# Mixing the state-space tiles of a group in one insertion, with the last keys in 64 masked rows and the root a step later

## The chip, the cores and the metric

One NeuronCore of a Trainium2 chip runs the kernel; the others are idle. The metric is the device time of one execution in microseconds (us), the median of several runs. TensorE (PE) multiplies into PSUM, VectorE (DVE) and ScalarE (ACT) do the elementwise work, GpSimd (POOL) sets constants up, and SyncE (SP) issues the DMAs that bring weights in.

## The reference

A two-layer trunk over 272 tokens (16 learned meta tokens ahead of 256) and a width of 2048. Layer 0 is a Mamba-2 mixer and a SwiGLU; layer 1 is a stick-breaking attention against a shared K/V and a SwiGLU. The change touches only the mixer's scan, which per chunk of the sequence computes

```python
cum = jnp.cumsum(dtc * A, axis=1)
seg = cum[:, :, None] - cum[:, None, :]
decay = jnp.exp(jnp.where(causal, seg, -jnp.inf))
cb = jnp.einsum("bqgn,bsgn->bqsg", cc, bc)
xdt = xc * dtc[..., None]
y_diag = jnp.einsum("bqsg,bqsgr,bsgrp->bqgrp", cb, decay, xdt)
y_off = jnp.einsum("bqgn,bgrpn->bqgrp", cc, state) * jnp.exp(cum)[..., None]
```

There are 8 groups of 8 heads of 64 channels, with a state of 128. Behind the scan each group is multiplied by a gate, divided by the root of its mean square (the "root" below) and sent through an output projection.

## The kernel before, in words

Everything is kept transposed, channels in partitions and tokens in the free dimension. A projection (`project`, L130) makes 128 output channels for all 272 tokens: it loads a piece of 8 weight blocks of 128x128 (`load`, L94, on SP's queue, 5 buffers), splits it into a rounded half `hi` on ScalarE (L105, 5 buffers) and the remainder `lo` on VectorE (L107, 4 buffers), and runs three matmuls of 272 columns per block (L120, L121, L122). With 16 blocks that is 48 matmuls, with the 8 blocks of an output projection 24. The result lies in one of four `pp` buffers of PSUM until VectorE takes it away (L163, or L166 for the residual).

The mixer's eight groups run one after another. `ssd_project` (L328) makes a group's six convolution tiles (B, C and four tiles of x; a projection, taps at L321 and L324, a Silu at L326) and four gate tiles `zs`. The scan itself, `ssd_scan` (L357), is a generator: it is put on a list, and `pump` (L196) runs it up to its next `yield` after each projection of the *next* group or, behind groups 3 and 5 and behind the last one, of an output projection. A group's projections give ten such steps. Within this, the Tile framework's scheduler decides the order in which each engine's instructions stand; each engine then runs its own list strictly in that order.

A scan's steps for a group (272 tokens in key blocks of 128, 128 and 16; the queries that a block reaches are `QRY`):

1. Loads of the decay's exponents (`et`, `elast`, `ef`, L379 and L398); the scores `pc` (L400 to L402); twelve transposes of the x tiles (L367), four for each key block, the last block's being 16 wide; the causal mask (L405 to L407).
2. to 5. The keys times their step size (`scaled`, L370), the decay by Relu and Exp on ScalarE (L386, L421 to L424), decay times scores (`mix`, L388).
6. and 7. The products, two of the four tiles in each step (L435): for a tile, four matmuls of a 64-wide half with 128 and 144 query columns and two with the 16 columns of the last keys (L440), which add up in one PSUM tile `py`, then one 128-wide matmul for the part of the carried state (L442). VectorE adds the parts and multiplies with the gate (L444 to L450), ScalarE squares (L177, L180), VectorE sums the squares in `ga` (L181).
8. The root: a matmul with ones (L188) that sums `ga` over partitions, Sqrt on ScalarE, a reciprocal on VectorE (L191).
9. The scaled result is split into two halves `y` for the output projection (L459 to L462).

`cum` and the step size `dt` are made once, ahead of group 0, transposed on PE (L293, L294) and kept as `cumT` and `dtT`; `cum` also goes to DRAM, whence the decay's exponents are broadcast.

Of the kernel before, what the change touches and what calls it, by code (L numbers as in the profile page):

```python
# [6 lines left out]
F32 = mybir.dt.float32  # L7
F32R = mybir.dt.float32r
AF = mybir.ActivationFunctionType
ALU = mybir.AluOpType  # L10
# [3 lines left out]
P = 128  # L14
# [3 lines left out]
META = 16  # L18
T = SEQ + META
G = 8  # L20
HPG = 8
HD = 64
NH = G * HPG
DI = 4096
GT = DI // G // P
# [4 lines left out]
WC = 8  # L30
LC = 8
BLK = [(0, 128), (128, 256), (256, 272)]
QRY = [(0, 128), (128, 272), (256, 272)]
OQ = 128
SCALE = 128 ** -0.5
NEG = -1e30
# [9 lines left out]
def trunk(tc, a, out):  # L46
    nc = tc.nc
    V, S, PE = nc.vector, nc.scalar, nc.tensor

    with tc.tile_pool(name="const", bufs=1) as cp, \  # L50
# [7 lines left out]
        h = cp.tile([P, KD, T], F32, name="h")  # L58
# [6 lines left out]
        gd = cp.tile([P, 2, 32], F32, name="gd")  # L65
# [23 lines left out]
        def nm(s):  # L89
            uid[0] += 1  # L90
            return f"{s}_{uid[0]}"
# [82 lines left out]
        def sumsq(acc, src, first):  # L174
            n = src.shape[-1]
            if first:
                S.activation(acc, src, AF.Square)  # L177
            else:
                sq = sp.tile([P, T], F32, tag="sq", name=nm("sq"))
                S.activation(sq[:, :n], src, AF.Square)  # L180
                V.tensor_tensor(out=acc, in0=acc, in1=sq[:, :n], op=ALU.add)  # L181
# [48 lines left out]
        with tc.tile_pool(name="ssd0", bufs=1) as q0, \  # L230
# [6 lines left out]
                V.memset(xi[:, :CONV - 1], 0.0)  # L237
                xins.append(xi)
            cumD = dp.tile([NH, T], F32, name="cumD")
            cumT = q0.tile([P, 3, NH], F32, name="cumT")  # L240
            dtT = q0.tile([P, 3, NH], F32, name="dtT")
            wT = q0.tile([P, NH], F32, name="wT")
            ybuf = [pair(q0, 2 * GT, T, PAD["y"], TP, name=f"y{i}") for i in range(2)]

            with tc.tile_pool(name="dtp", bufs=1) as dq:
# [40 lines left out]
                for b0, b1 in ((0, OQ), (OQ, T)):  # L286
                    V.tensor_tensor_scan(cum[:, b0:b1], one[:, :b1 - b0], da[:, b0:b1],
                                         0.0, ALU.mult, ALU.add)
                nc.sync.dma_start(cumD, cum)
                pt = ptp.tile([P, 512], F32, tag="pt", name=nm("pt"))  # L290
                for b, (b0, b1) in enumerate(BLK):
                    n = b1 - b0
                    PE.transpose(pt[:n, b * NH:(b + 1) * NH], cum[:, b0:b1], ident[:NH, :NH])  # L293
                    PE.transpose(pt[:n, (3 + b) * NH:(4 + b) * NH], dt[:, b0:b1], ident[:NH, :NH])  # L294
                for b, (b0, b1) in enumerate(BLK):
                    n = b1 - b0
                    V.tensor_copy(cumT[:n, b, :], pt[:n, b * NH:(b + 1) * NH])
                    V.tensor_copy(dtT[:n, b, :], pt[:n, (3 + b) * NH:(4 + b) * NH])
                pl = prp.tile([P, 512], F32, tag="pr", name=nm("pl"))
                PE.matmul(pl[:, :NH], sel, cumT[:, 0, :], start=True, stop=True)  # L300
                V.tensor_tensor(out=wT, in0=pl[:, :NH], in1=cumT[:, 0, :], op=ALU.subtract)
# [3 lines left out]
            q1 = ctx.enter_context(tc.tile_pool(name="ssd1", bufs=1))  # L305
            q2 = ctx.enter_context(tc.tile_pool(name="ssd2", bufs=2))
            cnt = [0]
            xlast = q1.tile([P, HPG, HD], F32, name="xlast")
            elast = [q1.tile([P, HPG, META], F32, name=f"elast{i}") for i in range(2)]
            for z in (xlast, *elast):  # L310
                nc.gpsimd.memset(z, 0.0)

# [41 lines left out]
            def head_bcast(t, n, g):  # L354
                return t[:n, HPG * g:HPG * (g + 1)].unsqueeze(2).to_broadcast([n, HPG, HD])

            def ssd_scan(g, bc, xc, zs):  # L357
                gh = slice(HPG * g, HPG * (g + 1))
                xd, gm = [None] * 3, [None] * 3


                def transposed(b, pool, tag):
                    b0, b1 = BLK[b]
                    n = b1 - b0
                    pt = pool.tile([P, 512], F32, tag=tag, name=nm("pt"))
                    for j in range(GT):
                        PE.transpose(pt[:n, j * P:(j + 1) * P], xc[:, j, b0:b1], ident)  # L367
                    return pt[:n].rearrange("p (h d) -> p h d", d=HD)

                def scaled(ph, t, n, tag):  # L370
                    x = xlast if n < P else q1.tile([P, HPG, HD], F32, tag=tag, name=nm("x"))
                    V.tensor_tensor(out=x[:n], in0=ph, in1=head_bcast(t, n, g), op=ALU.mult)
                    return x

                def load_decay(b):
                    (b0, b1), (c0, c1) = BLK[b], QRY[b]
                    n = b1 - b0
                    et = elast[g % 2] if n < P else q2.tile([P, HPG, c1 - c0], F32, tag="et", name=nm("et"))
                    nc.sync.dma_start(et[:n], cumD[gh, c0:c1].partition_broadcast(n))  # L379
                    gm[b] = et  # L380


# [3 lines left out]
                        S.activation(gm[b][:, i, :], gm[b][:, i, :], AF.Relu, scale=-1.0, bias=cumT[:, b, c:c + 1])  # L386

                def mix(b):  # L388
                    n = BLK[b][1] - BLK[b][0]
                    V.tensor_tensor(out=gm[b][:n], in0=gm[b][:n],  # L390
                                    in1=cbd[b].unsqueeze(1).to_broadcast(list(gm[b][:n].shape)), op=ALU.mult)

                for b in range(3):
                    load_decay(b)
                ef = q2.tile([P, GT, T - OQ], F32, tag="ef", name=nm("ef"), bufs=1)
                cv = cumD[gh, OQ:].rearrange("(j i) q -> i j q", i=2)
                for i in range(2):
                    nc.sync.dma_start(ef[i * HD:(i + 1) * HD], cv[i].partition_broadcast(HD))  # L398
                pc = pyp.tile([P, 512], F32, tag="py", name=nm("pc"))
                PE.matmul(pc[:, 0:272], bc[:, 0, 0:128], bc[:, 1, :], start=True, stop=True)  # L400
                PE.matmul(pc[:, 272:416], bc[:, 0, 128:256], bc[:, 1, 128:], start=True, stop=True)
                PE.matmul(pc[:16, 416:432], bc[:, 0, 256:], bc[:, 1, 256:], start=True, stop=True)  # L402
                ph = [transposed(0, ptp, "pt"), transposed(1, pyp, "py"), transposed(2, prp, "pr")]
                cb = q2.tile([P, 432], F32, tag="cb", name=nm("cb"), bufs=1)
                V.tensor_tensor(out=cb[:, 0:128], in0=pc[:, 0:128], in1=causal[:, :128], op=ALU.mult)  # L405
                V.tensor_tensor(out=cb[:, 272:416], in0=pc[:, 272:416], in1=causal, op=ALU.mult)
                V.tensor_tensor(out=cb[:16, 416:432], in0=pc[:16, 416:432], in1=causal[:16, :16], op=ALU.mult)  # L407
                S.copy(cb[:, 128:272], pc[:, 128:272])
                cbd = [cb[:, 0:128], cb[:, 272:416], cb[:16, 416:432]]
                fall(0)  # L410
                yield
                xd[0] = scaled(ph[0], dtT[:, 0], P, "xd0")
                xw = scaled(ph[0], wT, P, "xw")
                fall(1)
                e2 = gm[2][:META]
                V.tensor_tensor(out=e2, in0=e2, in1=cumT[:META, 2, gh].unsqueeze(2).to_broadcast(list(e2.shape)),
                                op=ALU.subtract)
                V.tensor_scalar(e2, e2, 0.0, None, ALU.min)
                yield
                xd[1] = scaled(ph[1], dtT[:, 1], P, "xd1")  # L420
                S.activation(gm[0], gm[0], AF.Exp, scale=-1.0)  # L421
                S.activation(gm[1], gm[1], AF.Exp, scale=-1.0)
                S.activation(e2, e2, AF.Exp)
                S.activation(ef, ef, AF.Exp)  # L424
                yield
                xd[2] = scaled(ph[2], dtT[:, 2], META, "xd2")
                mix(0)
                yield
                mix(1)
                mix(2)  # L430
                yield
                ga = sp.tile([P, T], F32, tag="ga", name=nm("ga"), bufs=1)


                for j0 in range(0, GT, 2):  # L435
                    pys = [pyp.tile([P, 512], F32, tag="py", name=nm("py")) for _ in range(2)]
                    for j, py in enumerate(pys, j0):
                        for b, (c0, c1) in enumerate(QRY):
                            for i in range(2):
                                PE.matmul(py[i * HD:(i + 1) * HD, c0:c1], xd[b][:, 2 * j + i, :],  # L440
                                          gm[b][:, 2 * j + i, :], start=b < 2, stop=b != 1)
                        PE.matmul(py[:, T:T + T - OQ], xw[:, 2 * j:2 * j + 2, :], cb[:, OQ:T], start=True, stop=True)  # L442
                    for j, py in enumerate(pys, j0):
                        V.tensor_tensor(out=ef[:, j, :], in0=py[:, T:T + T - OQ], in1=ef[:, j, :], op=ALU.mult)  # L444
                        yt = q2.tile([P, T], F32, tag="yt", name=nm("yt"))
                        c = GT * g + j
                        V.scalar_tensor_tensor(out=yt, in0=xc[:, j, :], scalar=gd[:, 0, c:c + 1], in1=py[:, :T],
                                               op0=ALU.mult, op1=ALU.add)
                        V.tensor_tensor(out=yt[:, OQ:], in0=yt[:, OQ:], in1=ef[:, j, :], op=ALU.add)
                        V.tensor_tensor(out=zs[:, j, :], in0=yt, in1=zs[:, j, :], op=ALU.mult)  # L450
                        sumsq(ga, zs[:, j, :], j == 0)
                    yield
                rg = sp.tile([P, T], F32, tag="rg", name=nm("rg"), bufs=1)
                rstd(rg, ga, DI // G)
                yield
# [289 lines left out]
```

## Time and profile before

| | us |
|---|---|
| median of 3 runs | 2666.77 (2666.76 to 2666.78) |
| the profiled execution | 2667.44 |
| its span, first to last instruction | 2665.7 |
| PE busy in the span | 2648.5 |
| DVE busy | 1608.8 |
| ACT busy | 1321.5 |
| mean granted TensorE clock | 0.998 |

A row of the timeline gives start and duration in us, engine, line, operation, what is written from what, and the shape; `x8` at the end means eight records merged. An fp32 matmul shows as two records, one for each of its passes. Since matmuls overlap, a duration is longer than the distance to the next start; the distances are what PE's stream costs. A row of the waits says which instruction waited for which: us in total, times, longest. A row by line gives the busy time and the mean in ns, then the idle time ahead of these instructions and what ended it. In a form like `128*64 128x144`, the weights are 128 rows by 64 columns and 144 columns pass through them.

### The profile page before, as it was taken

To read this page: it belongs to the slowest core of one execution; us is meant where nothing else is said; L and a number is where in the kernel's file an instruction comes from. 1 tells how busy PE (TensorE), PEld (TensorE's weight loads), DVE (VectorE), ACT (ScalarE), POOL (GpSimd) and SP (SyncE) were. 2 spreads that over 40 slices of the span, in tenths; PEclk is the share of its full clock that TensorE was granted. 3 is DMA by queue.
4 is the path that set the end of the run, shared out by engine and by line. 5 is a ranking of instruction groups with operands and counts; after the bars stand their busy time and mean duration, and the time that the engine had idled before them with its cause. 6 is when DMAs were issued, how large, how long until landed. Compare 5 with 4: busy or idle time off the path is not lost.

```text
span 2665.7 us, 52272 instructions
## 1 busy us (share of the span) xinstructions
PE 2648.5 (99%) x22118; PEld 2631.8 (99%) x22118; DVE 1608.8 (60%) x2236; ACT 1321.5 (50%) x1803; POOL 5.5 (0%) x22
## 2 busy tenths in 40 slices
PE   9999999999999999999999999999999999999998
PEld 9999999999999999999999999999999999999998
DVE  8777767767765555445555665555655555554554
ACT  7777565656544443334444554444544444443443
POOL 0000000000000000000000000000000000000000
PEclk9999999999999999999999999999999999999999
DMA  6655565555555555555555555555666666665664
GB/s 226 213 178 176 173 185 173 176 177 179 164 178 178 178 179 178 179 178 180 176 179 168 184 173 156 157 163 152 196 191 192 196 193 195 193 196 180 199 198 135
DMA packets 156234, 481.23 MB, mean 181 GB/s; under 512 B 18720, under 2 KB 39776, under 8 KB 156000
## 3 DMA queue, kind: packets, MB, share of 16 engines
q1 hardware_dynamic: 155712, 477.62, 57.7%
q8 instruction: 173, 2.83, 0.4%
q14 instruction: 61, 0.50, 0.1%
q10 hardware_dynamic: 288, 0.28, 0.0%
HBM read 475.67 MB, written 2.17 MB: 179 GB/s over the span
## 4 chain that ended last, share of the span: by engine, by line
PE 96%; ACT 1%; DVE 1%; DMA 1%; issue 0%; SPq 0%; DVEq 0%; ACTq 0%
PE pp L122 31%; PE pp L121 31%; PE pp L120 31%; DMA et<-cumD 1%; PE py L440 1%; PE py L442 0%; PE pt L367 0%; ACT hi L105 0%; PE psc L569 0%; PE po L595 0%; PE po L594 0%; PE pr L188 0%; ACT et L386 0%; DVE lo L107 0%; DVE ca L324 0%
## 5 line engine op out<-in xcount | busy, mean ns | idle before, releaser
L105 ACT CAST hi<-raw 128x1024 fp32r<-128x1024 f32 (+1 forms) x899 | 928.8, 1035 | 1157.8 <-PE pp L121 928.0
L107 DVE TENSOR_TENSOR lo<-raw,hi 128x1024 fp32r<-128x1024 f32 (+1 forms) x899 | 1075.4, 1198 | 445.5 <-PE pp L122 217.4
L120 PE MATMUL pp<-u,hi 128*128 128x272 f32 (+1 forms) x4064 | 1152.2, 284 | 0.4 <-ACT hi L105 0.4
L121 PE MATMUL pp<-u,hi 128*128 128x272 f32 (+1 forms) x4064 | 1150.8, 283 | 0.0
L122 PE MATMUL pp<-u,lo 128*128 128x272 f32 (+1 forms) x4064 | 1149.1, 283 | 0.0
L120 PEld LDWEIGHTS pp<-u,hi 128*128 128x128 f32 x4064 | 764.9, 188 | 0.8 <-ACT hi L105 0.6
L121 PEld LDWEIGHTS pp<-u,hi 128*128 128x128 f32 x4064 | 764.9, 188 | 0.4
L122 PEld LDWEIGHTS pp<-u,lo 128*128 128x128 f32 x4064 | 764.4, 188 | 0.6 <-DVE lo L107 0.2
L122 PE MATMUL pp<-hid,lo 128*128 128x272 f32 (+1 forms) x1408 | 396.0, 281 | 0.0
L120 PE MATMUL pp<-hid,hi 128*128 128x272 f32 (+1 forms) x1408 | 396.0, 281 | 0.0
L121 PE MATMUL pp<-hid,hi 128*128 128x272 f32 (+1 forms) x1408 | 396.0, 281 | 0.0
L120 PEld LDWEIGHTS pp<-hid,hi 128*128 128x128 f32 x1408 | 264.8, 188 | 0.0
L121 PEld LDWEIGHTS pp<-hid,hi 128*128 128x128 f32 x1408 | 264.8, 188 | 0.0
L122 PEld LDWEIGHTS pp<-hid,lo 128*128 128x128 f32 x1408 | 264.8, 188 | 0.0
L120 PE MATMUL pp<-ukv,hi 128*128 128x272 f32 x512 | 148.2, 289 | 0.0
L120 PE MATMUL pp<-y,hi 128*128 128x272 f32 x512 | 147.6, 288 | 0.0
L121 PE MATMUL pp<-y,hi 128*128 128x272 f32 x512 | 147.1, 287 | 0.0
L122 PE MATMUL pp<-ukv,lo 128*128 128x272 f32 x512 | 146.7, 287 | 0.0
L122 PE MATMUL pp<-y,lo 128*128 128x272 f32 x512 | 146.7, 287 | 0.0
L121 PE MATMUL pp<-ukv,hi 128*128 128x272 f32 x512 | 146.7, 287 | 0.0
L166 DVE TENSOR_TENSOR h<-pp,h 128x272 f32<-128x272 f32 (+1 forms) x128 | 55.7, 436 | 118.8 <-PE pp L122 118.0
L163 DVE TENSOR_TENSOR gt<-pp,rB 128x272 f32<-128x272 f32 (+1 forms) x88 | 38.1, 433 | 135.8 <-PE pp L122 135.7
(226 smaller groups left out, 2609.8 us busy)
## 6 DMA issues: line engine op xcount, KB each, us to landing
raw<-w_gu SPq DMA_DIRECT2D x352, 512.0 KB, 3.6
raw<-w_down SPq DMA_DIRECT2D x160, 512.0 KB, 3.6
raw<-w_in SPq DMA_DIRECT2D x152, 512.0 KB, 3.7
raw<-w_out SPq DMA_DIRECT2D x64, 512.0 KB, 3.9
raw<-w_kv SPq DMA_DIRECT2D x64, 512.0 KB, 3.6
raw<-w_q SPq DMA_DIRECT2D x32, 512.0 KB, 3.6
raw<-w_o SPq DMA_DIRECT2D x32, 512.0 KB, 3.6
raw<-w_down SPq DMA_DIRECT2D x32, 256.0 KB, 2.7
```

What stands on the lines that cost most here:

```text
L105: S.copy(hi[:, :n, :m], raw[:, :n, :m])
L107: V.tensor_tensor(out=lo[:, :n, :m], in0=raw[:, :n, :m], in1=hi[:, :n, :m].bitcast(F32), op=ALU.subtract)
L120: PE.matmul(ps[:, :n], wh, xl, start=first, stop=False)
L121: PE.matmul(ps[:, :n], wh, xh, start=False, stop=False)
L122: PE.matmul(ps[:, :n], wl, xh, start=False, stop=last)
L163: V.tensor_tensor(out=dst, in0=ps[:, :r.shape[-1]], in1=r, op=ALU.mult)
L166: V.tensor_tensor(out=hm, in0=ps[:, :hm.shape[-1]], in1=hm, op=ALU.add)
L440: PE.matmul(py[i * HD:(i + 1) * HD, c0:c1], xd[b][:, 2 * j + i, :], gm[b][:, 2 * j + i, :], start=b < 2, stop=b != 1)
```

## The change

The last 16 keys no longer have 16 rows of their own. Their scores are made four times over, from keys repeated in `ke`, in 64 rows, one for each x tile and key; a mask `own` (made on GpSimd) keeps in each row only the columns of its own tile. Their x values, copied to `xe`, are transposed in one transpose to 64 rows by 128 channels. `cumR` and `dtR` hold the step sizes for these rows. So two matmuls of 64 columns make the last keys' part of all four tiles, in columns 416 to 480 of the third tile, and VectorE adds it to `ef` in one operation.

All four tiles of a group are now multiplied in one step: all 64-wide matmuls first, then the last keys, then the four 128-wide ones. Two of the four PSUM tiles come from the `pp` pool. VectorE's work is in two steps, tiles 2 and 3 and then 0 and 1; one step without work of the scan follows, and then the root. A scan has ten steps instead of nine.

```diff
+                ke = q2.tile([P, P // META, META], F32, tag="ke", name=nm("ke"), bufs=1)
+                S.copy(ke, bc[:, 0, 256:].unsqueeze(1).to_broadcast([P, P // META, META]))
+                xe = q2.tile([P, GT, META], F32, tag="xe", name=nm("xe"), bufs=1)
+                S.copy(xe, xc[:, :, 256:])
-                PE.matmul(pc[:16, 416:432], bc[:, 0, 256:], bc[:, 1, 256:], start=True, stop=True)
-                ph = [transposed(0, ptp, "pt"), transposed(1, pyp, "py"), transposed(2, prp, "pr")]
+                PE.matmul(pc[:, 416:432], ke.rearrange("p r t -> p (r t)"), bc[:, 1, 256:], start=True, stop=True)
+                ph = [transposed(0, ptp, "pt"), transposed(1, pyp, "py")]
+                pl = prp.tile([P, 512], F32, tag="pr", name=nm("pt"))
+                PE.transpose(pl[:R, :P], xe.rearrange("p j t -> p (j t)"), ident)
...
-                for j0 in range(0, GT, 2):
-                    pys = [pyp.tile([P, 512], F32, tag="py", name=nm("py")) for _ in range(2)]
-                    for j, py in enumerate(pys, j0):
-                        for b, (c0, c1) in enumerate(QRY):
-                            for i in range(2):
-                                PE.matmul(py[i * HD:(i + 1) * HD, c0:c1], xd[b][:, 2 * j + i, :],
-                                          gm[b][:, 2 * j + i, :], start=b < 2, stop=b != 1)
-                        PE.matmul(py[:, T:T + T - OQ], xw[:, 2 * j:2 * j + 2, :], cb[:, OQ:T], start=True, stop=True)
+                pys = [pool.tile([P, 512], F32, tag=tag, name=nm("py"))
+                       for pool, tag in ((pyp, "py"), (pyp, "py"), (pp, "pp"), (pp, "pp"))]
+                for j, py in enumerate(pys):
+                    for b, (c0, c1) in enumerate(QRY):
+                        for i in range(2):
+                            PE.matmul(py[i * HD:(i + 1) * HD, c0:c1], xd[b][:, 2 * j + i, :],
+                                      gm[b][:, 2 * j + i, :], start=True, stop=True)
+                end = pys[2][:, 416:416 + R]
+                for i in range(2):
+                    PE.matmul(end[i * HD:(i + 1) * HD], xlast[:, i * HD:(i + 1) * HD], el[:, :, i, :], start=True, stop=True)
+                for j, py in enumerate(pys):
+                    PE.matmul(py[:, T:T + T - OQ], xw[:, 2 * j:2 * j + 2, :], cb[:, OQ:T], start=True, stop=True)
+                for j, py in enumerate(pys):
+                    V.tensor_tensor(out=ef[:, j, :], in0=py[:, T:T + T - OQ], in1=ef[:, j, :], op=ALU.mult)
+                V.tensor_tensor(out=ef[:, :, P:], in0=end.rearrange("p (j q) -> p j q", j=GT), in1=ef[:, :, P:],
+                                op=ALU.add)
+                for j in (2, 3, 0, 1):
...
+                    if j in (3, 1):
+                        yield
+                yield
                 rg = sp.tile([P, T], F32, tag="rg", name=nm("rg"), bufs=1)
                 rstd(rg, ga, DI // G)
```

New line numbers that the text uses: L421 to L423 are the scores (before L400 to L402), L379 and L426 the transposes, L464 and L468 the 64-wide products (L440), L470 the carried state's (L442), L472 to L481 VectorE's part (L444 to L450), L417 and L419 the copies `ke` and `xe`, L339 the convolution's Silu (L326), L494 the `y` casts (L461).

On TensorE, at the products of group 0, a pair of tiles stood like this before; 48 projection matmuls later the other pair followed in the same form:

```order
L440 MATMUL py_1496<-et_1103,x_1207 64x128 x2
L440 MATMUL py_1496<-et_1105,x_1289 64x144 x2
L440 MATMUL py_1496<-elast_730,xlast 64x16 x2
L442 MATMUL py_1496<-cb_1130,x_1209 128x144
L440 MATMUL py_1497<-et_1103,x_1207 64x128 x2
L440 MATMUL py_1497<-et_1105,x_1289 64x144 x2
L440 MATMUL py_1497<-elast_730,xlast 64x16 x2
L442 MATMUL py_1497<-cb_1130,x_1209 128x144
```

Now, from the third of the four tiles on:

```order
L464 MATMUL py_1508<-et_1110,x_1216 64x128 x2
L464 MATMUL py_1508<-et_1112,x_1298 64x144 x2
L464 MATMUL py_1509<-et_1110,x_1216 64x128 x2
L464 MATMUL py_1509<-et_1112,x_1298 64x144 x2
L468 MATMUL py_1508<-elast_737,xlast 64x64 x2
L470 MATMUL py_1506<-cb_1138,x_1218 128x144
L470 MATMUL py_1507<-cb_1138,x_1218 128x144
L470 MATMUL py_1508<-cb_1138,x_1218 128x144
L470 MATMUL py_1509<-cb_1138,x_1218 128x144
```

The 128-wide matmuls have moved from behind each tile to the end of all four, and the second insertion is gone. The root's matmul (L188) stood 52 projection matmuls behind the second pair; it stands 144 behind the one insertion, or 72 in group 7. From the root to the next group's scores there were 140 (528 where an output projection lies between); there are 96 (480), and 72 ahead of group 7 (before 116).

On VectorE, behind the products of group 0, this stood before (`ef`, `yt`, `zs` and `ga` are the scan's, `lo` the projections'):

```order
L107 TENSOR_TENSOR lo_1662<-raw_1658,hi_1660 128x1024
L444 TENSOR_TENSOR ef_1108<-py_1496,ef_1108 128x144
L447 SCALAR_TENSOR_TENSOR yt_1513<-xc_735,gd,py_1496 128x272
L444 TENSOR_TENSOR ef_1108<-py_1497,ef_1108 128x144
L449 TENSOR_TENSOR yt_1513<-yt_1513,ef_1108 128x144
L447 SCALAR_TENSOR_TENSOR yt_1519<-xc_735,gd,py_1497 128x272
L450 TENSOR_TENSOR zs_737<-yt_1513,zs_737 128x272
L449 TENSOR_TENSOR yt_1519<-yt_1519,ef_1108 128x144
L450 TENSOR_TENSOR zs_737<-yt_1519,zs_737 128x272
L107 TENSOR_TENSOR lo_1701<-raw_1697,hi_1699 128x1024
```

Now the part between two `lo` is longer; its last rows, behind four `ef` products, the addition to `ef` and the first two `yt` with their gates:

```order
L478 SCALAR_TENSOR_TENSOR yt_1617<-xc_742,gd,py_1506 128x272
L478 SCALAR_TENSOR_TENSOR yt_1624<-xc_742,gd,py_1507 128x272
L181 TENSOR_TENSOR ga_1505<-ga_1505,sq_1546 128x272
L480 TENSOR_TENSOR yt_1617<-yt_1617,ef_1115 128x144
L480 TENSOR_TENSOR yt_1624<-yt_1624,ef_1115 128x144
L481 TENSOR_TENSOR zs_744<-yt_1617,zs_744 128x272
L481 TENSOR_TENSOR zs_744<-yt_1624,zs_744 128x272
L107 TENSOR_TENSOR lo_1700<-raw_1696,hi_1698 128x1024
```

Eight operations stood between the two `lo`; eighteen stand there now, all four tiles at once.

On ScalarE, ahead of the scores and transposes of group 1, this stands now where the last convolution tile `xc_1039` is finished:

```order
L334 ACTIVATE ca_1831<-xin_467,cw 128x272
L494 CAST y_479<-zs_744 128x272 x4
L105 CAST hi_2043<-raw_2041 128x1024
L339 ACT_TABLE_LOAD
L339 ACTIVATE xc_1039<-ca_1831 128x272
L105 CAST hi_2073<-raw_2071 128x1024
L419 COPY xe_1930<-xc_1039 128x64
```

Before, the same Silu stood behind the group's exponentials, with the `y` casts well ahead of them:

```order
L461 CAST y_473<-zs_737 128x272 x4
L386 ACTIVATE et_1917<-et_1917,cumT 128x144
L105 CAST hi_1989<-raw_1987 128x1024
L326 ACT_TABLE_LOAD
L326 ACTIVATE xc_1032<-ca_1758 128x272
L386 ACTIVATE et_1917<-et_1917,cumT 128x144
L105 CAST hi_2036<-raw_2034 128x1024
L421 ACT_TABLE_LOAD
L421 ACTIVATE et_1915<-et_1915 128x1024
L321 ACTIVATE ca_1838<-xin_467,cw 128x272
```

The `y` casts of the group before have moved next to the last convolution tile, and a copy is new behind it. ScalarE's list has 44 table loads instead of 61. From the last output projection of the mixer on, all engines' lists are as before.

## What the change does to the time: the prediction

> **What bounds the kernel now.** I read the page's head, then who waits for whom, then TensorE's timeline around the state-space instructions.
>
> ```profile
> span 2665.7 us, 52272 instructions
> PE 2648.5 (99%) x22118; PEld 2631.8 (99%) x22118; DVE 1608.8 (60%) x2236; ACT 1321.5 (50%) x1803; POOL 5.5 (0%) x22
> ```
>
> TensorE (PE) works through the whole span; a busy PE is no proof of a useful one, since ends of matmuls are modelled, so I go by starts. The waits say who follows whom (us in total, times, longest):
>
> ```profile
> ACT hi L105 <- PE pp L121: 928.0, 632, 2.3
> DVE lo L107 <- PE pp L122: 217.4, 159, 2.3
> PEld pr L188 <- DVE ga L181: 5.5, 5, 1.5
> PEld pt L367 <- ACT xc L326: 1.3, 4, 0.4
> ```
>
> ScalarE and VectorE wait for PE to give back weight buffers; PE waits only 5.5 us for the root's sum and 1.3 us for the last convolution tile. So work taken off VectorE or ScalarE is worth nothing by itself, and time taken out of PE's stream is worth itself, as long as those two stay ahead. PE's timeline (start, duration, line) at the first two `py` insertions of group 0:
>
> ```profile
> 112.07 0.29 PE L122 MATMUL pp<-u,lo 128*128 128x272 f32 x1
> 112.29 0.69 PE L440 MATMUL py<-et,x 128*64 128x128 f32 x8
> 112.80 0.24 PE L440 MATMUL py<-elast,xlast 128*64 128x16 f32 x4
> 112.98 0.51 PE L442 MATMUL py<-cb,x 128*128 128x144 f32 x2
> 113.42 0.69 PE L440 MATMUL py<-et,x 128*64 128x128 f32 x8
> ...
> 114.11 0.51 PE L442 MATMUL py<-cb,x 128*128 128x144 f32 x2
> 114.36 0.38 PE L120 MATMUL pp<-u,hi 128*128 128x272 f32 x1
> 114.58 0.28 PE L121 MATMUL pp<-u,hi 128*128 128x272 f32 x1
> 114.71 0.29 PE L122 MATMUL pp<-u,lo 128*128 128x272 f32 x1
> ...
> 120.26 0.29 PE L122 MATMUL pp<-u,lo 128*128 128x272 f32 x1
> ...
> 122.77 0.28 PE L121 MATMUL pp<-u,hi 128*128 128x272 f32 x1
> ```
>
> The 45 projection steps from 114.71 to 120.26 give 0.123 us a step. From the last projection matmul before the insertion (112.07) to the second one after it (114.58) are 2.51 us, two steps of which are normal: the insertion costs 2.26 us. The second (120.26 to 122.77) costs the same, so a group pays 4.52 us, eight groups 36.2.
>
> The insertion of the score matmuls and transposes, in group 0 and, by its first and last starts, in group 1:
>
> ```profile
> 80.15 0.29 PE L122 MATMUL pp<-u,lo 128*128 128x272 f32 x1
> 80.28 0.62 PE L400 MATMUL pc<-bc 128*128 128x272 f32 x2
> 80.73 0.41 PE L401 MATMUL pc<-bc 128*128 128x144 f32 x2
> 81.07 0.21 PE L402 MATMUL pc<-bc 128*16 128x16 f32 x2
> 81.22 1.53 PE L367 MATMUL pt<-ident,xc 128*128 128x128 f32 x12
> 82.50 0.37 PE L120 MATMUL pp<-u,hi 128*128 128x272 f32 x1
> 82.71 0.29 PE L121 MATMUL pp<-u,hi 128*128 128x272 f32 x1
> 147.98 0.29 PE L122 MATMUL pp<-u,lo 128*128 128x272 f32 x1
> ...
> 149.05 1.84 PE L367 MATMUL pt<-ident,xc 128*128 128x128 f32 x12
> ...
> 150.86 0.28 PE L121 MATMUL pp<-u,hi 128*128 128x272 f32 x1
> ```
>
> Group 0 pays 2.56 less 0.25, 2.31 us; group 1 2.88 less 0.25, 2.63, where the twelve transposes take longer because the last tile comes late. Two passes of 272 columns take 0.45 us (80.28 to 80.73): 0.83 ns per column and pass. A transpose takes 1.28/12 = 0.107 us.
>
> **The change, part by part.** *One insertion for four tiles.* Before, a pair holds, by columns, per tile 2x(128+144) in the 64-wide form (its two halves run beside each other, eight records in 0.51 us) = 0.45 us, 2x16 = 0.03 and 2x144 of L442 = 0.24: 0.72, a pair 1.44. The insertion costs 2.26, so 0.82 is lost at the five places where the form changes (into 64-wide, to 128-wide, back, to 128-wide, out): 0.16 each, seen best at L442, 0.44 us for 0.24 of columns. A group has ten such changes; after, by the order, three: all L464, then L468, then all L470. Content after: 4x(0.45+0.24) plus 2x64 columns of the last keys (0.11) = 2.87; with 3x0.16, 3.35 us. Gain 1.17 a group, 9.4 us. Ends: if the 0.20 around each L442 stays, 2.87 + 4x0.20 and 0.40 for the ways in, out and past L468 give 4.07, a gain of 3.6 us in all; if a change costs only the 0.10 seen at 112.07 to 112.29 beyond a step, 10.4.
>
> The Trainium skill (TensorEngine Tiling (Array Packing), section Tiling Modes) says that changing the tiling mode drains the TensorE, while another tile of the same mode does not. The 0.44 us of L442 agrees.
>
> *Transposes and scores.* Twelve transposes become nine: 3x0.107 = 0.32 us. L402, two passes of 16 columns, holds PE from 80.97 (80.73 plus 0.24 of columns) to 81.22: 0.25 us for 0.03 of columns. Its replacement, 128 wide, needs no change of form but loads 128 weight columns twice; between 0.05 and 0.25 I take 0.15. Saved: 0.42 in groups 0, 4 and 6, where the convolution is long done. Groups 1, 2, 3 and 5 I take as group 1, 0.74 each, since the order now keeps the transposes in one piece. In group 7 it cuts them in three; I give nothing there. Sum 4.2. The 64-wide transpose of the last keys I charge with no change of form, since today's 16-wide ones keep the step of 0.107.
>
> New is a wait: L423 needs `ke`, L426 `xe`, both copied on ScalarE; behind L426 on PE stand the next projection's matmuls. `ke` is made long before. `xe` stands behind the last convolution's Silu and, in groups 1, 2, 3 and 5, one cast. ScalarE in group 1 now, with the durations I use:
>
> ```profile
> 137.93 1.37 ACT L461 CAST y<-zs 128x272 fp32r<-128x272 f32 x4
> 139.21 0.41 ACT L386 ACTIVATE et<-et,cumT 128x144 f32<-128x144 f32 x1
> 139.52 1.04 ACT L105 CAST hi<-raw 128x1024 fp32r<-128x1024 f32 x1
> 140.58 1.28 ACT L326 ACT_TABLE_LOAD   x1
> 141.88 0.43 ACT L326 ACTIVATE xc<-ca 128x272 f32<-128x272 f32 x1
> ```
>
> After, the root stands only 96 projection matmuls ahead of L421 (before 140). The last convolution's projection ends 48 steps, 5.9 us, ahead of L421. From there: evacuation and first tap some 1.0, four `y` casts 1.4 with up to 0.7 of waiting for VectorE, cast 1.0, table 1.3, Silu 0.4, cast 1.0, copy about 0.3: 7.1 us, so `xe` is there 1.2 us after L421 starts. PE wants it after 0.45+0.24+0.15 and eight transposes of 0.107, at 1.7. It should just fit; for a margin of 0.5 us I charge 0.2 in five groups, 1.0. Net 3.2 us; ends 0 and 4.2.
>
> *The root later.* It stood 52 projection steps after the second pair and came up to 1.5 us early:
>
> ```profile
> 128.94 0.29 PE L120 MATMUL pp<-u,hi 128*128 128x272 f32 x1
> 130.27 0.72 PE L188 MATMUL pr<-ga,ones 128*128 128x272 f32 x2 [1.05 <-DVE ga L181]
> ```
>
> Now all sums can start after one insertion, and the root stands 144 steps (17.8 us) behind it, 72 (8.9 us) in group 7. VectorE's share, rows by line (busy, mean ns):
>
> ```profile
> L107 DVE TENSOR_TENSOR lo<-raw,hi 128x1024 fp32r<-128x1024 f32 x197 | 238.4, 1215 | 36.3 <-issue 17.6 <-ACT hi L105 10.1 <-PE pp L122 8.4
> L447 DVE SCALAR_TENSOR_TENSOR yt<-xc,gd,py 128x272 f32<-128x272 f32 x32 | 15.7, 490 | 0.0
> L450 DVE TENSOR_TENSOR zs<-yt,zs 128x272 f32<-128x272 f32 x32 | 14.0, 438 | 0.6
> L181 DVE TENSOR_TENSOR ga<-ga,sq 128x272 f32<-128x272 f32 x24 | 10.5, 437 | 7.3 <-ACT sq L180 7.1
> L444 DVE TENSOR_TENSOR ef<-py,ef 128x144 f32<-128x144 f32 x32 | 9.7, 302 | 0.7
> ```
>
> Nine operations like L444 (four products, four additions, one more for the end; the last is narrower, so at most this), four L447, four L450, three L181: 2.7+2.0+1.8+1.3 = 7.8 us. With the casts between, that ends well inside 17.8, and in group 7 about at 8.9. Gain 5.5, less 0.3 for group 7: 5.2; ends 3 and 5.5.
>
> *Start.* On PE the transposes of `cum` move 16 projection steps (2.0 us) earlier, and on VectorE the first convolutions leave the chain that makes `cum`, for they now come after it. I charge 0.3; ends -0.3 and 2.0. Those convolutions then have some 18 us until L421.
>
> *At nothing.* ScalarE and VectorE lose and gain small operations, the broadcast of the last keys has 64 rows for 16, SP's loads stand behind it as before: all covered by the 928 and 217 us in which they wait for PE. Two `py` tiles sit in the projections' buffers. The projection two further on needs the first back 48 steps on at the earliest (5.9 us, output projection); L478 frees it after four products, one addition and two yt, 2.5 us. If that cover went, PE would wait for the difference.
>
> Sum: 9.4+3.2+5.2-0.3 = 17.5. The profiled execution took 2667.44 us (span 2665.7), so 2649.9; the median shown lies 0.67 below it: **2649.3 us**.
>
> **The rivals.** *The last tile late* (15%). ScalarE runs later than I count, as the sums did when the root came up to 1.5 us early. If `xe` is 1.8 us later, PE waits 1.3 in five groups, 6.5 instead of 1.0: gain 12.0, 2654.8 us. For it: 0.5 us of margin. Against: seventeen table loads of 1.28 us fewer in ScalarE's order.
>
> *A change of form is not the price* (8%). Then L442 keeps its 0.20 and the merging gives 3.6: gain 11.7, 2655.1 us. Against: L401, the same columns without a change, takes 0.34 to L402, of which L402's narrow form has part; L442 takes 0.44.
>
> *The 64-wide transpose changes the form twice* (6%), into 64-wide and out: 0.32 us a group, 2.6 in all: gain 14.9, 2651.9 us. Against: the four 16-wide transposes of a group lie in the 1.28 us of twelve, with no step left over. The skill's page on tiling stands on both sides: its drain rule (Tiling Modes) would charge it, its section Restrictions and Gotchas says that column tiling excludes fp32 transposes.
>
> *The root still waits* (5%), because the squares on ScalarE, not VectorE, were late: gain 12.3, 2654.5. Against: 44 steps more.
>
> *Slower: VectorE's burst starves PE* (3%). Between two weight casts VectorE now does 18 operations, 6.9 us; the next cast ends 8.1 us after the insertion. Four casts ahead cover 4x24 steps, 11.8 us: 3.7 to spare. If the burst also waits 8 us for ScalarE's squares, PE stalls 4.3 us in each group, 34 us: 2683 us; it decides from 3.7 us of waiting on, and is slower than before from 5.9. Against: all such waits of L181 now sum to 7.1 us. The skill's page on tiling warns of this in its section Performance Considerations: tiling speeds TensorE, not the evacuation of PSUM.
>
> **How the numbers follow.** My forecast has 63%, mostly within 2646 to 2653 us; with the second form of the transpose that is 69%. The range must reach to the three rivals near 2655: 2645.5 to 2655.5. The best ends (10.4+4.2+5.5) give 2646.0. A difference of 0.2% (5.3 us) is what a measurement of this kernel can tell from none; faster by that has 0.94, within it 0.03 (several rivals together), slower 0.03.
>
> **What would show it.** Right: one `py` insertion a group of about 3.4 us from L464 to the projection; L470 steps near 0.12 us after the first; no wait of L188 but in group 7; an L421 insertion near 1.9 us. Wrong: L426 waiting for `xe` in five groups; L470 steps above 0.2; projection matmuls waiting for VectorE's `lo` some 12 us after the insertion; `cum` late by 2 us. Should the time lie above 2661, one of these must cost over 12 us.

## The result, and the profile after

The changed kernel took 2650.05 us (median of four runs, 2649.46 to 2651.82) beside 2666.77 for the kernel before (2665.33 to 2666.78): a ratio of 0.9939, 95% interval 0.9927 to 0.9952. That is 16.7 us less; the forecast was 17.5 less, 2649.3 us. The profiled execution after is the slowest of its four, 2651.82 us with a span of 2649.8.

The head of the page after, and TensorE's waits (us in total, times, longest):

```profile
span 2649.8 us, 52061 instructions
PE 2635.0 (99%) x21998; PEld 2625.3 (99%) x21998; DVE 1607.1 (61%) x2244; ACT 1301.8 (49%) x1810; POOL 5.7 (0%) x25
```
```profile
PE pt L379 <- ACT xc L339: 2.0, 2, 1.7
...
PE pt L306 <- DVE cum L297: 0.6, 1, 0.6
PE pt L426 <- ACT xe L419: 0.3, 1, 0.3
```

The wait of the root (L188) for its sum is gone from the list in all groups; the last group had none before and has none now. New is a wait for the last convolution tile, 2.0 us in two places, and a small one for `xe`. A busy PE still says nothing, so the reading goes by starts again: what an insertion costs is the time from the last projection matmul ahead of it to the second one behind it, less two steps of 0.123 us.

TensorE's timeline at the products of group 0, now in one piece:

```profile
112.30 0.28 PE L122 MATMUL pp<-u,lo 128*128 128x272 f32 x1
112.52 2.07 PE L464 MATMUL py<-et,x 128*64 128x128 f32 x32
114.42 0.28 PE L468 MATMUL py<-elast,xlast 128*64 128x64 f32 x4
114.63 1.25 PE L470 MATMUL py<-cb,x 128*128 128x144 f32 x8
115.62 0.38 PE L120 MATMUL pp<-u,hi 128*128 128x272 f32 x1
115.84 0.29 PE L121 MATMUL pp<-u,hi 128*128 128x272 f32 x1
```

From 112.30 to 115.84 are 3.54 us, less 0.25: 3.30, the same in all eight groups. Four L470 take 0.99 us (114.63 to 115.62), 0.25 each, where of the two L442 of a pair before the first held TensorE for 0.44; the second, with the projection behind it, held it for 0.25 (114.11 to 114.36).

The scores and transposes of group 1 (first and last starts), where nothing waits, and of group 3, where two things do:

```profile
145.67 0.29 PE L122 MATMUL pp<-u,lo 128*128 128x272 f32 x1
145.80 0.62 PE L421 MATMUL pc<-bc 128*128 128x272 f32 x2
...
147.78 0.29 PE L121 MATMUL pp<-u,hi 128*128 128x272 f32 x1
```
```profile
275.35 0.29 PE L122 MATMUL pp<-y,lo 128*128 128x272 f32 x1
...
277.09 0.76 PE L379 MATMUL pt<-ident,xc 128*128 128x128 f32 x5 [0.24 <-ACT xc L339]
278.17 0.30 PE L426 MATMUL pt<-ident,xe 128*64 128x128 f32 x1 [0.32 <-ACT xe L419]
...
278.43 0.29 PE L121 MATMUL pp<-y,hi 128*128 128x272 f32 x1
```

Group 1 pays 2.11 less 0.25, 1.86 us; group 3 pays 3.08 less 0.25, 2.83. In group 7 it is worse:

```profile
627.49 0.29 PE L122 MATMUL pp<-y,lo 128*128 128x272 f32 x1
...
631.16 0.44 PE L379 MATMUL pt<-ident,xc 128*128 128x128 f32 x2 [1.73 <-ACT xc L339]
...
632.16 0.43 PE L121 MATMUL pp<-y,hi 128*128 128x272 f32 x1
```

From 627.49 to 632.16 are 4.67 us with five projection steps (0.62) in them, so 4.05; and behind it the projection itself runs slowly for a while. The stretches around it (length, busy time and count of each engine, then the granted clock, the DMA share and GB/s):

```profile
632.00:635.20 3.20, 3.20 (x16) 3.20 (x16) 3.20 (x6) 0.47 (x2) 0.00 (x0) 0.52 0.02 5
635.20:640.00 4.80, 4.80 (x41) 4.80 (x40) 3.65 (x6) 2.06 (x2) 0.00 (x0) 1.00 0.38 116
```

The clock is 0.52 for three microseconds; thirteen steps take 0.226 us instead of 0.123, 1.3 us in all. So group 7 pays 5.4 us where it paid 2.5.

Added up in this way, against the terms of the forecast (us gained; the second profile of the same program comes from the experiments below):

| term | forecast | first profile | second profile |
|---|---|---|---|
| products, 16 x 2.265 to 8 x 3.297 | 9.4 | 9.9 | 9.9 |
| scores and transposes, eight groups | 3.2 | 0.4 | 2.7 |
| roots, eight groups, 9.4 to 3.7 | 5.2 | 5.7 | 5.7 |
| start (`cum`), 1.6 to 2.3 and 2.5 | -0.3 | -0.7 | -0.9 |
| sum | 17.5 | 15.3 | 17.4 |

The spans say the same: 2665.7 to 2649.8 is 15.9, and to the second profile's 2648.2 it is 17.5.

### The profile page after: what moved, and what is told of

It is laid out like the page before. It is cut to its first block, busy times and chain, and to the rows that moved or that the text cites. A ratio compares the mean times of both kernels' runs of the same rounds, so it can differ in the third digit from the quotient of the medians.

```text
span 2649.8 us, 52061 instructions
## 1 busy us (share of the span) xinstructions
PE 2635.0 (99%) x21998; PEld 2625.3 (99%) x21998; DVE 1607.1 (61%) x2244; ACT 1301.8 (49%) x1810; POOL 5.7 (0%) x25
## 4 chain that ended last, share of the span: by engine, by line
PE 96%; ACT 2%; DVE 1%; DMA 1%; issue 1%; DVEq 0%; SPq 0%; ACTq 0%
PE pp L120 31%; PE pp L122 31%; PE pp L121 31%; PE py L464 1%; DMA et<-cumD 0%; ACT hi L105 0%; ACT et L397 0%; PE psc L602 0%; PE py L470 0%; PE po L628 0%; PE po L627 0%; PE pt L379 0%; DVE lo L107 0%; PE pr L188 0%; DMA raw<-w_first 0%
```

## The experiments

The first four take the terms apart; the others follow the one that fell short.

**The step alone.** One empty step ahead of the root, in the kernel before:

```diff
+                yield
                 rg = sp.tile([P, T], F32, tag="rg", name=nm("rg"), bufs=1)
```

> The kernel before, with one empty step of the scan put ahead of the root (L455); nothing else of the change. My step of the sum: the eight roots of before take 9.4 us over normal steps, of which 3.7 (8 x 0.46) is their own work, so 5.2 to 5.7 us go and nothing is late in their place: about 2661.3 us, a ratio of 0.998. Rival, from the trace of after: the step also moves the four y casts beside the next group's last convolution, and it is this that made the transposes of groups 3 and 7 wait and the clock fall to 0.52 behind the wait in group 7; then the waits appear here too, on xc in L367 (about 1.0 in group 3, 2 to 4 in group 7, 1.4 for the clock), and take the gain of the roots back: 2665 to 2667 us.

Measured: 2661.85 us beside 2666.47, ratio 0.9983 (0.9974 to 0.9992), 4.6 us less. In its trace all eight roots cost 0.46, so 5.7 are gone as expected. The rival has a small part: group 7's scores go from 2.5 to 3.6, by a wait of 1.04 us for the last tile, while in groups 1, 2, 3 and 5 the transposes lose the 0.25 to 0.3 they had waited. No step is slow behind it. So the step earns what the forecast said. It alone does not bring group 3's loss; in group 7 it brings 1.1 us, where the kernel after loses 1.6 in the first profile, without the slow clock, and 0.8 in the second.

**The step kept in the last group only**, in the kernel after:

```diff
-                yield
+                if g == G - 1:
+                    yield
                 rg = sp.tile([P, T], F32, tag="rg", name=nm("rg"), bufs=1)
```

> The kernel after, with the empty step ahead of the root kept in the last group alone. If the step is what made the last convolution late for the transposes: the insertions at L421 of groups 3 and 7 come to some 1.9 us (after: 2.8 and 6.0), no matmul runs at half clock behind group 7's, and the roots still wait for nothing, since group 0's last sum ended 12.0 us behind the start of the insertion and the root now stands 3.3 + 96 x 0.123 = 15.1 behind it: gain on after 1.0 + 4.1 + 1.4 = 6.5, about 2643.5 us. Rival (the copy xe or the one insertion makes the last tile late, not the step): groups 3 and 7 as in after, 2650 us. Second rival: roots come early again, L188 waits for ga in groups 0 to 6 by some 0.5 us each: 2647 us.

Measured: 2650.75 us, ratio 0.9942 (0.9929 to 0.9954): no gain on after. The second rival falls, no root waits. Group 7 fell to 3.06 and its clock stayed at 1.0, but group 3 kept 2.91, and groups 1 and 2, which had not waited, now paid 2.30, because `xe` was done 0.5 us later there. So of the waits only group 7's can be the step's. How much of it is not settled here: 3.06 is 1.0 less than in the first profile, but 0.3 less than in the second, and those two profiles of one program differ by 0.7 themselves. What stands ahead of group 3's last tile here, on ScalarE (L421 starts at 276.43):

```profile
274.71 1.28 ACT L447 ACT_TABLE_LOAD   x1
276.01 0.31 ACT L447 ACTIVATE elast<-elast 64x128 f32<-64x128 f32 x1
276.33 1.28 ACT L339 ACT_TABLE_LOAD   x1
277.63 0.43 ACT L339 ACTIVATE xc<-ca 128x272 f32<-128x272 f32 x1
```

The Exp of the last keys, 0.31 us long, stands between the Silus of two convolution tiles and costs two loads of the table: 2.9 us right ahead of the tile that TensorE waits for. This Exp is not new. Before, with 16 rows, it took as long, but it stood behind group 3's scores, which started at 283.93:

```profile
288.97 0.31 ACT L423 ACTIVATE elast<-elast 16x128 f32<-16x128 f32 x1
```

That it now comes ahead of them was the next theory.

**The pairs sorted**, in the kernel before:

```diff
                                 PE.matmul(py[i * HD:(i + 1) * HD, c0:c1], xd[b][:, 2 * j + i, :],
                                           gm[b][:, 2 * j + i, :], start=b < 2, stop=b != 1)
+                    for j, py in enumerate(pys, j0):
                         PE.matmul(py[:, T:T + T - OQ], xw[:, 2 * j:2 * j + 2, :], cb[:, OQ:T], start=True, stop=True)
```

> The kernel before, with the two L442 of each pair set behind all 64-wide products of the pair; the same work, five changes of form a pair become three. If a change of form costs 0.16 us: 16 pairs x 2 x 0.16 = 5.1 us less, of which the root may give back up to 0.3 a group (the first tile's addition can start later): 2661.6 to 2664 us, insertions of 1.94 us instead of 2.265. Rival (L442's time is its own, not that of a change): 2666.8, insertions of 2.26.

Measured: 2662.67 us, ratio 0.9987 (0.9978 to 0.9996). The first insertion of group 0:

```profile
112.24 0.29 PE L122 MATMUL pp<-u,lo 128*128 128x272 f32 x1
...
113.73 0.76 PE L443 MATMUL py<-cb,x 128*128 128x144 f32 x4
...
114.45 0.28 PE L121 MATMUL pp<-u,hi 128*128 128x272 f32 x1
```

2.21 less 0.25, 1.96 us instead of 2.265: 0.31 for two changes of form fewer, 4.9 us in all sixteen, of which the roots took back 0.6 (their sum is 10.0 instead of 9.4). The rival is out: the same matmuls in another order cost less.

**The tiles mixed**, in the kernel after:

```diff
                     for b, (c0, c1) in enumerate(QRY):
...
+                    PE.matmul(py[:, T:T + T - OQ], xw[:, 2 * j:2 * j + 2, :], cb[:, OQ:T], start=True, stop=True)
                 end = pys[2][:, 416:416 + R]
...
-                for j, py in enumerate(pys):
-                    PE.matmul(py[:, T:T + T - OQ], xw[:, 2 * j:2 * j + 2, :], cb[:, OQ:T], start=True, stop=True)
```

> The kernel after, with each tile's product L470 put right behind its own four L464; the same work in one insertion, with ten changes of form instead of three. If a change costs 0.16 us: 7 x 0.16 = 1.12 us a group, 9.0 in all: 2659 us, insertions of 4.4 us instead of 3.3. Rival (the gain of the merging came from having one insertion a group instead of two, the way in and out, at some 0.6 a group, and not from the forms): insertions of 3.3 to 3.4, 2650 us.

Measured: 2663.21 us, ratio 0.9988 (0.9979 to 0.9997), 13 us over the kernel after. The insertion of group 0 (L466 is the carried state's product here):

```profile
112.31 0.28 PE L122 MATMUL pp<-u,lo 128*128 128x272 f32 x1
112.53 0.68 PE L464 MATMUL py<-et,x 128*64 128x128 f32 x8
113.14 0.51 PE L466 MATMUL py<-cb,x 128*128 128x144 f32 x2
113.58 0.69 PE L464 MATMUL py<-et,x 128*64 128x128 f32 x8
...
117.25 0.29 PE L121 MATMUL pp<-u,hi 128*128 128x272 f32 x1
```

4.94 less 0.25, 4.69 us: 1.39 a group more than sorted, 11.1 in all, and L466 is back at 0.44 (113.14 to 113.58). One insertion with mixed forms costs more than the two of before (4.53), so putting the four tiles together earns nothing by itself; the order in it does. The other 2 us of the 13 are later tiles: the insertions for the scores sum to 18.9 us here, to 17.1 in the second profile of after.

**The last keys' price**, by leaving them out. In the kernel before, the four products of 16 columns in each tile; in the kernel after, L468 and the addition of its result:

```diff
-                        for b, (c0, c1) in enumerate(QRY):
+                        for b, (c0, c1) in enumerate(QRY[:2]):
...
-                                          gm[b][:, 2 * j + i, :], start=b < 2, stop=b != 1)
+                                          gm[b][:, 2 * j + i, :], start=True, stop=True)
```
```diff
-                for i in range(2):
-                    PE.matmul(end[i * HD:(i + 1) * HD], xlast[:, i * HD:(i + 1) * HD], el[:, :, i, :], start=True, stop=True)
...
-                V.tensor_tensor(out=ef[:, :, P:], in0=end.rearrange("p (j q) -> p j q", j=GT), in1=ef[:, :, P:],
-                                op=ALU.add)
```

> The kernel before without the four products of 16 columns (the last 16 keys) in each tile; it leaves out the share of the last 16 keys in y. My sum gave them their columns alone, 0.03 us a tile: then a pair's insertion falls from 2.265 to 2.2. Rival, from the row of the kernel with sorted pairs, where the first tile's four stand between products of the same width and hold TensorE from 112.97 to 113.06: 0.09 us a tile or more, a pair 2.09 or less.

> The kernel after without the two products L468 of the last keys and the addition L473 of their result; it leaves out the share of the last 16 keys in y. My sum gave the two 0.11 us of columns; the rows of after hold TensorE from 114.42 to 114.63 for them: if that is their price the insertion falls from 3.297 to 3.09, if the columns alone are, and the rest is the change of form behind them, to 3.19.

The insertions of group 0, of before without these products and of after without L468:

```profile
112.03 0.29 PE L122 MATMUL pp<-u,lo 128*128 128x272 f32 x1
...
114.39 0.29 PE L121 MATMUL pp<-u,hi 128*128 128x272 f32 x1
```
```profile
112.15 0.28 PE L122 MATMUL pp<-u,lo 128*128 128x272 f32 x1
...
115.58 0.28 PE L121 MATMUL pp<-u,hi 128*128 128x272 f32 x1
```

2.36 less 0.25 is 2.11, a pair's 2.265 less 0.15: 0.075 us a tile, between the two expectations. 3.43 less 0.25 is 3.18: the two L468 cost 0.11, their columns. The times, 2664.06 and 2647.28 us in one run each, are not used.

**The Exp held back**, in the kernel after: a column of zeros made from the scores (`cl`), so that the Exp cannot stand ahead of them.

```diff
+                zero = q2.tile([P, 1], F32, tag="zero", name=nm("zero"), bufs=1)[:R]
+                V.tensor_scalar(zero, cl[:, 0, 0:1], 0.0, None, ALU.mult)
...
-                S.activation(e2, e2, AF.Exp)
+                S.activation(e2, e2, AF.Exp, bias=zero)
```

> The kernel after, with the Exp of the last keys (L447) held behind the scores by a bias column of zeros made from cl; one small VectorE operation a group more. In the trace of after this Exp stands on ScalarE between the Silus of groups 1, 2, 3 and 5's last two convolution tiles and brings two loads of the table with it (1.28 + 0.31 + 1.28 us). Theory: it is what makes the last tile late in group 3, where a weight cast more stands ahead; then the insertion at L421 falls from 2.83 to 1.86 us there, xe is copied some 2.9 us earlier in groups 1, 2 and 5 as well, and group 7, where the Exp stands elsewhere, stays at 4.0: 1.0 us less than after, 2649.1 us. Rival: the four y casts and the weight cast make it late; then group 3 stays at 2.8 and the time is that of after.

Measured: 2649.47 us (2648.78 to 2649.74), ratio 0.9936 (0.9924 to 0.9949). ScalarE ahead of group 3's scores in the kernel after (L421 starts at 275.48), and then with the Exp held (275.99):

```profile
270.96 1.28 ACT L447 ACT_TABLE_LOAD   x1
272.25 0.31 ACT L447 ACTIVATE elast<-elast 64x128 f32<-64x128 f32 x1
...
275.31 1.28 ACT L339 ACT_TABLE_LOAD   x1
276.60 0.43 ACT L339 ACTIVATE xc<-ca 128x272 f32<-128x272 f32 x1
...
277.87 0.24 ACT L419 COPY xe<-xc 128x64 f32<-128x64 f32 x1
```
```profile
273.60 1.05 ACT L105 CAST hi<-raw 128x1024 fp32r<-128x1024 f32 x1
275.35 0.43 ACT L339 ACTIVATE xc<-ca 128x272 f32<-128x272 f32 x1 [0.70 <-DVE ca L337]
275.76 0.42 ACT L496 CAST y<-zs 128x272 fp32r<-128x272 f32 x1
276.08 0.24 ACT L419 COPY xe<-xc 128x64 f32<-128x64 f32 x1
```

`xe` comes 2.4 us behind the start of L421 in the one and 0.1 behind it in the other. Group 3's insertion is 1.86, as all others of groups 0 to 6, and group 7 has 3.2. The scheduler has moved other work too: three of the four y casts still stand ahead of the last Silu, with three weight casts where there were two, and the weight cast between the Silu and `xe` has gone behind `xe`. So the y casts and the weight casts are not what made the tile late. The run without L468 agrees: its Exp stands far from this Silu (231.30 and 294.07, the Silu at 274.01), and its group 3 pays 1.86 as well. The cause of group 3's wait is shown. The time is 0.4 us over that expected; as a gain on the kernel after on the same chip (2649.88, below) 0.4 us is less than these runs can tell.

**Both edits**, the Exp held and the step in the last group only:

> Both edits: the empty step kept in the last group alone, and the Exp of the last keys held behind the scores. With the step alone the insertions at L421 took 2.30, 2.30, 2.91 and 3.06 us in groups 1, 2, 3 and 7, against 1.86 without a wait; there the Exp with its two loads stands right before the last Silu (from 2.8 us before L421 to 0.1 behind it). If the Exp is the cause, groups 1, 2 and 3 fall to 1.86, 1.9 us in all, and group 7 keeps its 3.06 (its last Silu follows another's): 2648.8 us, a ratio to before of 0.9935 or less. Rival (the y casts and the tap order hold the tile): 2650.7 as with the step alone.

Measured: 2649.03 us (2648.40 to 2649.39), ratio 0.9935 (0.9922 to 0.9947). Groups 1, 2 and 3, which had paid 2.30, 2.30 and 2.91 with the step's edit alone, are at 1.86, so the Exp was the cause there too; group 7 fell further than expected, to 2.53. It is the best version: its insertions for the scores sum to 15.6 us, those of the second profile of after to 17.1.

**The kernel after once more**, on the same chip as the two before and the next:

> The kernel after once more, as the measure for the other three and to see whether the clock falls again. If the wait of 2 us in group 7 lowers the clock each time, the matmuls behind it run at 0.227 us a step again for some 3 us; if that was chance, they run at 0.123 and the span is 1.4 us shorter than in the first profile. The time: 2650 us.

Measured: 2649.88 us (2649.36 to 2650.26), ratio 0.9938 (0.9924 to 0.9951). Group 7 waits again, but for less, and the steps behind it are of 0.12 us:

```profile
630.80 0.44 PE L379 MATMUL pt<-ident,xc 128*128 128x128 f32 x2 [1.18 <-ACT xc L339]
...
631.74 0.29 PE L122 MATMUL pp<-y,lo 128*128 128x272 f32 x1
631.87 0.28 PE L120 MATMUL pp<-y,hi 128*128 128x272 f32 x1
```

Its group 7 pays 3.3 us and its group 3 2.6. Of the two profiled executions of this kernel only the first shows the slow clock. With both edits the kernel is 0.85 us faster than this, with ranges that all but part; the intervals of the ratios overlap, so the time alone does not settle it.

**The wait filled**, in the kernel after:

```diff
+                        if g == G - 1 and b == 0 and j == GT - 1:
+                            fill = prp.tile([P, 512], F32, tag="pr", name=nm("fill"))
+                            for i in range(16):
+                                PE.matmul(fill[:, :P], xc[:, 2, 0:P], ident, start=True, stop=True)
                         PE.transpose(pt[:, j * P:(j + 1) * P], xc[:, j, b0:b1], ident)
```

> The kernel after, with sixteen matmuls of no use (128 x 128, from a finished convolution tile, into a buffer that nobody reads) between the transposes of the third and the last tile of group 7, where TensorE waits. They fill about 1.7 us of the 2 us. If standing idle lowered the clock, no step behind the insertion takes 0.227 us any more and the insertion keeps its length: up to 1.4 us less than after in those executions in which the clock falls. Rival (the clock falls for something else): the slow steps are there again.

Measured: 2651.43 us, ratio 0.9945 (0.9932 to 0.9957). The experiment missed its aim:

```profile
628.76 3.74 PE L382 MATMUL fill<-ident,xc 128*128 128x128 f32 x32
632.33 0.71 PE L383 MATMUL pt<-ident,xc 128*128 128x128 f32 x5
```

Such a matmul shows as two records and takes 0.22 us (3.57 for sixteen), twice the 0.11 of a transpose, so the sixteen filled 3.6 us, and the insertion came to 5.4. No step behind it is slow, but none was in the kernel after on this chip either: it says nothing of what lowered the clock.

## Why the prediction was right, point by point

*What bounds the kernel.* Right. All that was gained was taken out of TensorE's list, and the sums by starts meet the spans within 0.6 us. That the total came so close is in part luck: the products and the roots earned 1.0 us more than the sum gave them, the scores 0.5 to 2.8 and the start 0.4 to 0.6 less.

*One insertion for four tiles, 9.4.* The size is right (9.9), the split of it was not. The step that counted "2x16 = 0.03" for a tile's last keys was too low: leaving them out freed 0.075. Their new form cost what was counted, 0.11 a group. So the last keys earned 32 x 0.075 - 8 x 0.11 = 1.5 us where the sum gave 0.1, and the changes of form earned 8.4 where it gave 9.3; the two errors stand against each other. The count of those changes was also off by the way out to the projection, which has the same width (the second L442 of a pair held TensorE for its 0.25 alone, in the prediction's own rows): by width there are 8 a group before, 2 after, 4 with sorted and 10 with mixed tiles. One then costs 0.31/2 = 0.15 (sorted), 1.39/8 = 0.17 (mixed), and in the insertion without last keys 0.21 if its products are taken as 4 x 0.69 of columns (3.18 less 2.76, over two), 0.15 if they are taken by the rows of after (1.90 for four tiles of L464 and 0.99 for L470). The upper end given as 10.4 comes to 10.8 by its own terms, 4.52 less 2.87 and 3 x 0.10, eight times; the 2646.0 further on goes with 10.8. The rival "a change of form is not the price" is out; the drain that the Trainium skill names (TensorEngine Tiling (Array Packing), section Tiling Modes) fits these rows. Whether the time goes into a drain or into the load of the next weights was not taken apart.

*Transposes and scores, 3.2.* This is the step that failed, and it is where the two profiles differ. The sizes without a wait were right: 2.32 to 1.86 is 0.45 in groups 0, 4 and 6 (forecast 0.42), and 0.76, 0.76 and 0.67 in groups 1, 2 and 5 (forecast 0.74 less 0.2); in these three groups `xe` was done 1.6 to 1.7 us behind the start of L421, forecast 1.2, and TensorE took it at 1.75, forecast 1.7, so it just fitted. Two places were wrong. Group 3 lost 0.04 to 0.24 instead of gaining: the prediction put all of ScalarE's small operations "at nothing", covered by the 928 us in which it waits for PE. An average hides nothing at one place. The Exp of the last keys, behind the scores before, now stood in front of the last Silu with two loads of the table; holding it back gave back all of the loss. And group 7, "I give nothing there", lost 0.8 and in the first profile 2.9, of which 1.3 are the slow clock. There the root's steps and the y casts of group 6 stand right ahead of the last tile: without the step 3.06, without the Exp as well 2.53, next to the 2.5 of before; single profiles, with 0.7 between two of one program. In the last of these two weight casts, 1.98 us together, stand right ahead of the last Silu; what holds the remaining 0.7 was not taken apart.

*The root later, 5.2.* Right: 5.7, shown by the step alone. The last group, for which 0.3 was taken off, does not wait, nor did it before.

*Start, -0.3.* -0.7 and -0.9, inside the ends given. The first transpose of `cum`, moved ahead, waits for its scan (0.6 us in the first profile, 0.3 before). This was read, not tried.

*At nothing, the rest.* The two tiles in the projections' buffers, the broadcast of the last keys and the longer burst on VectorE cost nothing that shows; no projection waits for `lo` behind an insertion. So the slower rival did not come.

*The rivals.* "The last tile late" was named with the right resource and the wrong places: five groups through `xe`, where it came to be two, first through the tile itself. Against what the sum had for these two, 0.54 gained and 0.2 lost, they cost 1.2 us more in the second profile and 3.5 in the first. The margin of 0.5 us shrank to 0.03 to 0.16 but held; in group 3 the cause was an instruction whose place had been put at nothing. "The 64-wide transpose" is out: group 1 pays 1.86, with no room for 0.32.

## What to carry to other kernels

Matmuls of two widths are worth sorting before they are worth merging: the same products cost 3.3 us sorted and 4.7 mixed, and mixed in one place they were dearer than in two. An engine that is idle for half of the span still has places where it is on the path: of each operation that an edit adds there, ask what stands behind it in its list and who waits for that, and count the loads of the activation table on both sides of it. A wait that a scheduler's order causes may be found by a false dependence that holds the suspect back, as the column of zeros did here.

## What the runs showed of the hardware

TensorE's granted clock fell to half for 3.41 us (631.66 to 635.07) right behind a wait of 1.73 us in one execution, and not behind one of 1.18 us at the same place. In all twelve traces the stretches from one change of this clock to the next are whole multiples of 3.41 us, and the wait of 1.73 us lay wholly in the 3.41 us ahead of the fall. The Trainium skill (TensorE: Matmul & The Clock Gate, section What's actually happening) puts the half rate behind an idle window of about 3.4 us; here less idle time was enough once. What decides it stays open.

A switch of ScalarE's table cost its load and nothing more: the cast ahead ends at 270.94, the load at 270.96 takes 1.28 us and the Exp starts at 272.25. The Trainium skill (ScalarE: Activation LUTs, section What ACT_TABLE_LOAD costs) has the same 1283 ns and a drain of 1380 ns beside it, which no row here shows.
